# Moving background modulation work between the stages of a one-core decoder layer, and another order of weight rooms in its double gate blocks

## The chip, the cores and the metric

One Trainium2 chip, of which the kernel uses one core. The metric is the time of one execution on the device in microseconds (us). The median of three runs of the kernel before is 1582.16 us.

## The reference

One layer of a decoder trunk for T = 256 tokens of width D = 2048, all in float32. Cut to what matters here:

```
mod = silu(c) @ w_ada + b_ada                  # 2048 x (6 x 2048)
shift1, scale1, gate1, shift2, scale2, gate2 = split(mod, 6)
h = rms_norm(x, norm1_gain) * (1 + scale1) + shift1
proj = h @ w_in                                # q/k/v of three mixers, r, a, and 3 x 2048 gate columns
o_sb  = stick_breaking_attention(q_sb, k_sb, v_sb)         # 6 heads of 128
o_dil = dilated_mixture(q_dil, k_dil, v_dil)               # 3 groups of 2 heads
o_gla = rms_norm(gla_chunked(q, k, v, log_a)) * silu(r)    # 4 heads, value width 256
g = sigmoid(gate columns)                      # 3 x 2048
y = g[0] * (o_sb @ w_br_sb) + g[1] * (o_dil @ w_br_dil) + g[2] * (o_gla @ w_br_gla)
x = x + gate1 * (y @ w_out)
h = rms_norm(x, norm2_gain) * (1 + scale2) + shift2
x = x + gate2 * (swiglu(h, w_ffn_in) @ w_ffn_out)
```

The layer needs shift1 and scale1 at once, gate1 only behind w_out, shift2 and scale2 only at the second norm, gate2 only at the end. So their share of the product with w_ada can be computed at any time before that. This late share is called the background modulation.

## The kernel before

**Products.** Each large product is made of three fp32r matmuls (lines 173 to 175): activations and weights are split into a high part and the rest. A weight tile `raw` (512 KB: two k of 128 rows by 512 columns) is loaded by SP's queue. ScalarE casts it to `whi` (line 165, in pairs line 236), VectorE subtracts to get `wlo` (line 166, in pairs line 222), and TensorE runs twelve matmuls of 512 columns on it, for two halves of the tokens. There are four tiles each of raw, whi and wlo, so the loads, casts and subtractions run some tiles ahead of TensorE. SP, ScalarE and VectorE each work through one queue in order.

**Order.** The program is written block by block, and a planner then lays down the order of each engine's instructions; work inside `prio()` is put earlier than it is written. At run time the order on each engine is fixed.

**Stages** (times of the profiled execution). First groups of k with the first norm, to 239 us. Last group (`LAST`, five k): thirteen projection blocks `proj_block(LAST, b)` of 512 columns, and among them the norms of q and k (`qk_norm`, squares at line 771, product at line 779), their transposes (`qk_turn`, lines 791 and 792), stick-breaking attention (matmuls at line 843, which take what ScalarE makes at line 838), and gated linear attention (line 867 and behind). A projection block is seeded with the earlier groups' sum (copy at line 620) and brought back by a copy (line 632). Two blocks for r to about 419 us. Three gate blocks of the first 512 columns with the dilated mixture, to 493 us. Three double gate blocks `gate_pair` (two times 512 columns each), 494 to 615 us. y blocks 0 to 2 (branch products times gates) to 684, three single gate blocks and y block 3 to 790, three w_out blocks to 850, the fourth with the second norm, then the feed-forward part to the end.

**Double gate blocks.** `fast_products` runs eight pairs of k. Three of them (`GATE_PAIRS`) are fast: seven products in place of eight, from sums of activations (`sums_of_h`) and sums of weights, which VectorE makes at line 222 as well. A split takes its rooms by turns: first those of `more_rooms` (extra tiles whose owners are idle), then the ordinary four whi/wlo. A9/A10 are such extra rooms and hold part of the gated linear output until the transposes of line 1261 have read it; X1/X2 are scratch of `sums_of_h`.

**Background.** `background()` is a generator over three segments (shift2, gate1, scale2). A step issues one load of w_ada on SP (line 517, 512 KB: one k by 1024 columns) into a tile of a ring (`ring["tags"]`: AR0, AR1, and in some stages KC, KD, OD), and where the ring is full it first issues the oldest multiply-add on VectorE ("mac", lines 419 and 421), placed behind the latest split. There are 96 loads and 96 macs. `block` ticks at every second k, `fast_products` twice per pair of k:

```
tick(state["rate"] * pace)         # line 189, pace is 1 in these blocks
tick(2 * state["rate"])            # fast_products, once per pair of k
```

`tick` adds up the rate, and makes a step for each whole number reached. So `state["rate"]` sets how many loads and macs a stage carries; what is left before the second norm is done at once. `RATE_IN` holds from projection block 5, `RATE_MID` from the r blocks, `RATE_LAST` from the last gate blocks. After the background come twelve k of gate2 (`gate2_bg`), beside w_out and the first feed-forward units.

Of the kernel before, what the change touches and what calls it, by code (L numbers as in the profile page):

```python
# [29 lines left out]
N_DIL = 6  # L30
N_GLA = 4
SEG_SHIFT1, SEG_SCALE1, SEG_GATE1, SEG_SHIFT2, SEG_SCALE2, SEG_GATE2 = range(6)
RATE_FIRST, RATE_IN, RATE_MID, RATE_PAIRS, RATE_Y, RATE_LAST = 0.8, 0.8, 0.6, 0.2, 0.5, 0.7

RATES_OP, RATES_FFN, RATE_OUT = (0.9, 0.7, 0.0), (0.75, 0.9, 0.7, 0.6), 0.5
GATE2_CUT = 12
LOOK = 3
DEFER = 4
# [42 lines left out]
def trunk(ctx: ExitStack, tc: tile.TileContext, I, out):  # L81
# [16 lines left out]
    def S(tag, shape, dtype=F32):  # L98
        return slot.tile(shape, dtype, tag=tag, name=nm(tag))
# [7 lines left out]
    def acc_bank(shape=None):  # L107
        return psa.tile(shape or [P, NB], F32, tag="acc", name=nm("acc"))
# [4 lines left out]
    @contextmanager  # L113
    def prio(offset=AHEAD):

        with tc.high_priority(offset=offset):
            start = tc.cur_priority
            yield
            n = tc.cur_priority - start
        tc.cur_priority += n  # L120

    state = {"rate": 0.0}
# [54 lines left out]
    def block(pss, act, src, k0, k1, c0, base=0, w=None, tiles=range(NT), go_on=False, more=False, seeded=False,  # L177
              steps=None, pace=None):

        if w is None:
            w = load_weights(src, k0, k1, c0)
        if pace is None:
            pace = 1.0 if tiles[-1] == NT - 1 else 0.0
        for k in range(k0, k1):
            if (k - k0) % 2 == 0:
                tick(state["rate"] * pace)
            if k - k0 == DEFER and later:  # L190
                with tc.issue_after(state["mm"].ins), prio():
                    later.pop()()
            if steps and k - k0 in steps:
                with tc.issue_after(state["mm"].ins), prio():
                    steps[k - k0]()
            wh, wl = w[k - k0]
            for t in tiles:
                h, l = act(base + k, t)
                mm3(pss[t], h, l, wh, wl, k == k0 and not go_on, k == k1 - 1 and not more, seeded)
# [411 lines left out]
    def proj_block(g, b, w=None, carry=False, steps=None):  # L611
        k0, k1 = GROUPS[g]
        go_on = bool(carried)
        pss = carried.pop() if go_on else [acc_bank() for _ in range(NT)]
        seeded = g == LAST and not go_on
        if seeded:

            with prio():
                for t in range(NT):
                    nc.scalar.copy(pss[t], A[b][:, t, :])  # L620
            go_on = True
        block(pss, h_at, w_in, k0, k1, b * NB, w=w, go_on=go_on, more=carry, seeded=seeded, steps=steps)
        if carry:
            carried.append(pss)
            return
        with prio():
            first = A[b] is None
            if first:
                A[b] = S(f"A{b}", [P, NT, NB])
            for t in range(NT):  # L630
                if first or seeded:
                    nc.scalar.copy(A[b][:, t, :], pss[t])
                else:
                    nc.vector.tensor_add(A[b][:, t, :], A[b][:, t, :], pss[t])
# [126 lines left out]
    def qk_norm(parts):  # L761

        n = sum(h1 - h0 for _, h0, h1, _ in parts)
        ss = small([P, NT, n])
        places, o = [], 0
        for b, h0, h1, _ in parts:
            for t in range(NT):
                for h in range(h0, h1):
                    junk = scr([P, P])
                    i = o + h - h0  # L770
                    nc.scalar.activation(junk, heads(b)[:, t, h, :], AF.Square, accum_out=ss[:, t, i : i + 1])
            places.append(slice(o, o + h1 - h0))
            o += h1 - h0
        r = rsqrt(ss.rearrange("p t h -> p (t h)"), 1.0 / P, [P, NT * n])
        r = r.rearrange("p (t h) -> p t h", t=NT)
        for (b, h0, h1, _), c in zip(parts, places):
            for t in range(NT):
                v = heads(b)[:, t, h0:h1, :]
                nc.vector.tensor_tensor(
                    v, v, r[:, t, c].unsqueeze(2).to_broadcast([P, h1 - h0, P]), op=ALU.mult  # L780
                )
# [269 lines left out]
    def mixture_rows(prob, sm, lse, den, spans):  # L1051
        G = lambda x, g: x[:, :, 2 * g : 2 * g + 2]
        coef = const.tile([P, NT, N_DIL], F32, name="dcoef")
        for g in range(3):
            nc.vector.tensor_mul(G(coef, g), G(sm, g), den)
        nc.vector.reciprocal(coef, coef)
        nc.vector.tensor_mul(coef, coef, lse)
        for h in range(N_DIL):
            p = prob[h // 2][:, h % 2, :]
            for t, (a, b) in enumerate(spans):  # L1060
                state["rows"] = nc.vector.tensor_scalar(p[:, a:b], p[:, a:b], coef[:, t, h : h + 1], None, op0=ALU.mult)
# [73 lines left out]
    def background():  # L1135
        for seg in (SEG_SHIFT2, SEG_GATE1, SEG_SCALE2):
            if seg == SEG_GATE1:
                acc = biased([S(f"T{4 + j}", [P, 2 * NB]) for j in range(2)], seg)
                yield from ada_segment_steps(acc, seg, rows_of("gate1", seg, acc), False)
            else:  # L1140
                acc = S("ada", [P, D])
                yield from ada_segment_steps(halves(acc), seg, columns(seg, acc))
        yield from last_macs()

    bg.append(background())
    state["rate"] = RATE_FIRST
    for b in range(0, 3):
        proj_block(LAST, b)
    state["rate"] = 0.0
    qk_norm(sb_parts)  # L1150
    for b in range(3, 5):
        proj_block(LAST, b)
# [32 lines left out]
    def gate_block(n, br, steps=None):  # L1185
        pss = [acc_bank() for _ in range(NT)]
        c0 = COL_G + br * D + n * NB
        block(pss, h_at, w_in, 0, KC, c0, steps=steps)
        g = S(gtags[n][br], [P, NT, NB])
        with prio():  # L1190
            for t in range(NT):
                if n == 0:
                    nc.scalar.copy(g[:, t, :], pss[t])
                else:
                    nc.scalar.activation(g[:, t, :], pss[t], AF.Sigmoid)
        gates[n, br] = g

    def gate_pair(br, own, other, rooms, raws=()):
        state["more_rooms"], state["more_raws"] = rooms, raws
        c0 = COL_G + br * D + NB  # L1200
        o = fast_products(w_in, c0, c0 + NB, GATE_PAIRS, h_at, h_sums, own, other, ("A0", "A1"), look=LOOK)
        with prio():
            for i in range(2):
                g = S(gtags[1 + i][br], [P, NT, NB])
                for t in range(NT):
                    nc.scalar.activation(g[:, t, :], o[i][t], AF.Sigmoid)
                gates[1 + i, br] = g
# [20 lines left out]
    with prio():  # L1228
        groups = dil_weights()
        mixture_rows(*groups)  # L1230
    gate_block(0, 0)
    ring["tags"] = ("AR0", "AR1", "KC", "KD")
    od, turns = mixture(groups[0])
# [86 lines left out]
    h_sums = sums_of_h()  # L1320
    state["rate"] = RATE_PAIRS
    ring["tags"] = ("AR0", "AR1", "KD")
    gate_pair(0, acc_bank, misc_bank, (("A9", "A10"), ("X1", "X2")))
    gate_pair(1, misc_bank, acc_bank, (("A9", "A10"),), ("X2",))
    gate_pair(2, acc_bank, misc_bank, (("A9", "A10"),))
    ring["tags"] = ("AR0", "AR1", "KC", "KD")
    state["rate"] = RATE_Y
# [339 lines left out]
```

## Time and profile before

| what | before |
|---|---|
| runs | 1583.51, 1582.16, 1581.06 us; median 1582.16 |
| profiled execution | 1581.34 us |
| its span, first to last instruction | 1579.5 us |
| mean granted TensorE clock | 0.999 |
| loads of w_ada into AR0/AR1 | 62 of 512 KB, 5.0 us from issue to landing |
| loads of w_in | 202 of 512 KB, 5.0 us |
| HBM traffic over the span | 254 GB/s |

Lines of the profile name an engine (PE is TensorE, PEld its weight load, DVE VectorE, ACT ScalarE, POOL GpSimd, SPq the queue of SyncE), the line of the kernel, the operation, output<-inputs and shape. In a timeline the first number is the start and the second the duration in us; in brackets at its end stands the idle time before it and what ended it. Starts of matmuls are measured, their ends are modelled, so that a matmul of 0.39 us overlaps the next. In a list of waits the three numbers are the total, the count and the longest, in us.

### The profile page before, as it was taken

The numbers are of one execution on the slowest core, as the hardware profiler recorded it, in microseconds if no ns is written. First come the engines' busy times: TensorE is split into PE (matmuls) and PEld (weight loads), VectorE is DVE, ScalarE is ACT, GpSimd is POOL, SyncE is SP. The second block draws the span as 40 slices with busy tenths as digits, with TensorE's granted clock in tenths as the row PEclk, the third lists the DMA queues.
The fourth block names the chain that finished last, engine by engine and source line by source line (L and its number), as shares of the span: only waits on it lengthen the run. The fifth ranks groups of instructions, "written<-read, shape, count | busy, mean of one in ns | idle before, by whom it ended". The sixth has DMA issues, their size and how long they took to land.

```text
span 1579.5 us, 20270 instructions
## 1 busy us (share of the span) xinstructions
PE 1562.7 (99%) x7177; PEld 1291.9 (82%) x7177; DVE 1407.3 (89%) x1728; ACT 881.9 (56%) x1222; POOL 12.3 (1%) x24
## 2 busy tenths in 40 slices
PE   9999999999999999999999999999999999999998
PEld 7878888788887888888887888888888888888887
DVE  6889997888888899987887889999999999889896
ACT  5654448875765555344434645556565555455553
POOL 1000000000000000000000000000000000000000
PEclk9999999999999999999999999999999999999999
DMA  9999988767778677888998896665566566866664
GB/s 334 359 327 322 336 305 289 252 214 226 253 249 269 217 239 243 304 285 310 315 315 276 305 314 222 196 206 198 191 211 211 173 200 231 289 227 201 225 209 138
DMA packets 196317, 402.26 MB, mean 255 GB/s; under 512 B 13102, under 2 KB 28116, under 8 KB 196216
## 3 DMA queue, kind: packets, MB, share of 16 engines
q1 hardware_dynamic: 194952, 397.75, 74.5%
q0 software_dynamic: 1088, 3.16, 0.5%
q8 instruction: 56, 0.92, 0.2%
q14 instruction: 45, 0.37, 0.1%
q10 hardware_dynamic: 176, 0.07, 0.0%
HBM read 395.68 MB, written 5.24 MB: 254 GB/s over the span
## 4 chain that ended last, share of the span: by engine, by line
PE 83%; DVE 7%; DMA 4%; ACT 3%; issue 2%; SPq 0%; ACTq 0%; DVEq 0%
PE acc L175 20%; PE acc L174 19%; PE acc L173 19%; PE misc L173 7%; PE misc L175 7%; PE misc L174 7%; DMA raw<-w_in 2%; DVE wlo L222 1%; ACT whi L165 1%; DVE wlo L166 1%; PE misc L945 1%; DMA A<-w_ada 1%; DMA OS<-w_ada 1%; DVE KD L222 1%; DVE OD L222 1%
## 5 line engine op out<-in xcount | busy, mean ns | idle before, releaser
L165 ACT CAST whi<-raw 128x1024 fp32r<-128x1024 f32 (+1 forms) x277 | 278.9, 1012 | 284.2 <-PE acc L175 149.8
L166 DVE TENSOR_TENSOR wlo<-raw,whi 128x1024 fp32r<-128x1024 f32 (+1 forms) x277 | 321.0, 1169 | 83.8 <-ACT whi L165 82.3
L173 PE MATMUL acc<-whi,H 128*128 128x512 f32 (+1 forms) x993 | 388.6, 392 | 1.0 <-ACT H L588 0.8
L174 PE MATMUL acc<-wlo,H 128*128 128x512 f32 (+1 forms) x993 | 387.5, 390 | 1.4 <-DVE wlo L166 1.3
L175 PE MATMUL acc<-whi,H 128*128 128x512 f32 (+1 forms) x993 | 387.2, 391 | 0.5 <-DVE H L595 0.4
L174 PEld LDWEIGHTS acc<-wlo,H 128*128 128x128 f32 x993 | 186.6, 188 | 40.1 <-DVE wlo L166 2.7
L175 PEld LDWEIGHTS acc<-whi,H 128*128 128x128 f32 x993 | 186.2, 188 | 40.0 <-DVE H L595 1.4
L173 PEld LDWEIGHTS acc<-whi,H 128*128 128x128 f32 x993 | 186.5, 188 | 39.7 <-ACT H L588 1.3
L236 ACT CAST whi<-raw 128x1024 fp32r<-128x1024 f32 (+1 forms) x144 | 138.9, 975 | 85.7 <-PE acc L175 41.2
L222 DVE TENSOR_TENSOR wlo<-raw,whi 128x1024 fp32r<-128x1024 f32 (+1 forms) x144 | 159.6, 1122 | 13.2 <-ACT whi L236 11.8
L175 PE MATMUL acc<-whi,A 128*128 128x512 f32 x217 | 84.5, 389 | 0.0
L174 PE MATMUL acc<-wlo,A 128*128 128x512 f32 x209 | 81.5, 390 | 1.5 <-DVE wlo L166 1.5
L173 PE MATMUL acc<-whi,A 128*128 128x512 f32 x209 | 81.8, 391 | 0.0
L173 PE MATMUL misc<-whi,H 128*128 128x512 f32 (+1 forms) x208 | 81.0, 389 | 0.0
L175 PE MATMUL misc<-whi,H 128*128 128x512 f32 (+1 forms) x208 | 80.6, 387 | 0.0
L174 PE MATMUL misc<-wlo,H 128*128 128x512 f32 (+1 forms) x208 | 80.5, 387 | 0.0
L421 DVE SCALAR_TENSOR_TENSOR ada<-AR,csil,ada 128x1024 f32<-128x1024 f32 x41 | 52.0, 1279 | 10.7 <-DMA AR<-w_ada 10.7
L222 DVE TENSOR_TENSOR A<-raw,A 128x512 f32<-128x512 f32 (+2 forms) x61 | 55.2, 912 | 0.7 <-ACT A L236 0.2
L175 PEld LDWEIGHTS acc<-whi,A 128*128 128x128 f32 x217 | 40.7, 188 | 8.5
L174 PEld LDWEIGHTS acc<-wlo,A 128*128 128x128 f32 x209 | 39.3, 188 | 10.0 <-DVE wlo L166 2.0
L173 PEld LDWEIGHTS misc<-whi,H 128*128 128x128 f32 x208 | 39.1, 188 | 8.3 <-issue 0.4
L173 PEld LDWEIGHTS acc<-whi,A 128*128 128x128 f32 x209 | 39.2, 188 | 8.0
(665 smaller groups left out, 3005.7 us busy)
## 6 DMA issues: line engine op xcount, KB each, us to landing
raw<-w_in SPq DMA_DIRECT2D x202, 512.0 KB, 5.0
raw<-w_ffn_in SPq DMA_DIRECT2D x135, 512.0 KB, 4.6
raw<-w_ffn_out SPq DMA_DIRECT2D x73, 512.0 KB, 5.4
AR<-w_ada SPq DMA_DIRECT2D x62, 512.0 KB, 5.0
raw<-w_out SPq DMA_DIRECT2D x32, 512.0 KB, 6.5
OS<-w_ada SPq DMA_DIRECT2D x24, 512.0 KB, 6.3
AR<-w_ffn_in SPq DMA_DIRECT2D x22, 512.0 KB, 5.4
KC<-w_ada SPq DMA_DIRECT2D x20, 512.0 KB, 5.6
```

The lines of the kernel that those rows point to most:

```text
L165: state["cast"] = nc.scalar.copy(hi[:, :n, :], raw[:, :n, :])
L166: state["split"] = nc.vector.tensor_tensor(lo[:, :n, :], raw[:, :n, :], hi[:, :n, :].bitcast(F32), op=ALU.subtract)
L173: nc.tensor.matmul(ps, lh, rh, start=start, stop=False, skip_group_check=seeded)
L174: nc.tensor.matmul(ps, lh, rl, start=False, stop=False, skip_group_check=seeded)
L175: state["mm"] = nc.tensor.matmul(ps, ll, rh, start=False, stop=stop, skip_group_check=seeded)
L222: done = nc.vector.tensor_tensor(dst, x, y, op=ALU.subtract)
L236: nc.scalar.copy(hi[:, :n, :], src)
L421: nc.vector.scalar_tensor_tensor(acc, raw, c, acc, op0=ALU.mult, op1=ALU.add)
L945: nc.tensor.matmul(ps[:n, t * N_GLA + h, :].rearrange("p (s l) -> p s l", l=L), at(f, h, t)[:, :n], odd(at(f, h, t)), start=True, stop=True,)
```

## The change

Three things. The background starts with projection block 5 (the sixth) and no longer with block 0. The rates of four stages differ: the three single gate blocks get a rate of their own (0.75 for 0.6), the pairs 0.3 for 0.2, y blocks 0 to 2 0.6 for 0.5, the w_out blocks (0.8, 0.4, 0) for (0.9, 0.7, 0). And each double gate block begins its turn of rooms behind the extra ones, so that its first four splits use the ordinary whi/wlo; in the first of them X1/X2 come ahead of A9/A10.

```
-RATE_FIRST, RATE_IN, RATE_MID, RATE_PAIRS, RATE_Y, RATE_LAST = 0.8, 0.8, 0.6, 0.2, 0.5, 0.7
-RATES_OP, RATES_FFN, RATE_OUT = (0.9, 0.7, 0.0), (0.75, 0.9, 0.7, 0.6), 0.5
+RATE_IN, RATE_MID, RATE_GATES, RATE_PAIRS, RATE_Y, RATE_LAST = 0.8, 0.6, 0.75, 0.3, 0.6, 0.7
+RATES_OP, RATES_FFN, RATE_OUT = (0.8, 0.4, 0.0), (0.75, 0.9, 0.7, 0.6), 0.5
...
     bg.append(background())
-    state["rate"] = RATE_FIRST
     for b in range(0, 3):
         proj_block(LAST, b)
-    state["rate"] = 0.0
     qk_norm(sb_parts)
...
     def gate_pair(br, own, other, rooms, raws=()):
         state["more_rooms"], state["more_raws"] = rooms, raws
+        state["tiles"] = len(rooms) - 1
...
+    state["rate"] = RATE_GATES
     gate_block(0, 0)
...
-    gate_pair(0, acc_bank, misc_bank, (("A9", "A10"), ("X1", "X2")))
+    gate_pair(0, acc_bank, misc_bank, (("X1", "X2"), ("A9", "A10")))
     gate_pair(1, misc_bank, acc_bank, (("A9", "A10"),), ("X2",))
     gate_pair(2, acc_bank, misc_bank, (("A9", "A10"),))
```

More of the change, by code (lines that the diff above doesn't have):

```diff
@@ L32 @@
 SEG_SHIFT1, SEG_SCALE1, SEG_GATE1, SEG_SHIFT2, SEG_SCALE2, SEG_GATE2 = range(6)
-RATE_FIRST, RATE_IN, RATE_MID, RATE_PAIRS, RATE_Y, RATE_LAST = 0.8, 0.8, 0.6, 0.2, 0.5, 0.7
-RATES_OP, RATES_FFN, RATE_OUT = (0.9, 0.7, 0.0), (0.75, 0.9, 0.7, 0.6), 0.5
+RATE_IN, RATE_MID, RATE_GATES, RATE_PAIRS, RATE_Y, RATE_LAST = 0.8, 0.6, 0.75, 0.3, 0.6, 0.7
+RATES_OP, RATES_FFN, RATE_OUT = (0.8, 0.4, 0.0), (0.75, 0.9, 0.7, 0.6), 0.5
 GATE2_CUT = 12
@@ L1145, in trunk @@
     bg.append(background())
-    state["rate"] = RATE_FIRST
     for b in range(0, 3):
         proj_block(LAST, b)
-    state["rate"] = 0.0
     qk_norm(sb_parts)
@@ L1199, in gate_pair @@
         state["more_rooms"], state["more_raws"] = rooms, raws
+        state["tiles"] = len(rooms) - 1
         c0 = COL_G + br * D + NB
@@ L1230, in trunk @@
         mixture_rows(*groups)
+    state["rate"] = RATE_GATES
     gate_block(0, 0)
@@ L1322, in trunk @@
     ring["tags"] = ("AR0", "AR1", "KD")
-    gate_pair(0, acc_bank, misc_bank, (("A9", "A10"), ("X1", "X2")))
+    gate_pair(0, acc_bank, misc_bank, (("X1", "X2"), ("A9", "A10")))
     gate_pair(1, misc_bank, acc_bank, (("A9", "A10"),), ("X2",))
```

## The prediction

> **What bounds the kernel now.** I read the head of the page first: the busy sums, then the chain that ended last, then the groups.
>
> ```profile
> span 1579.5 us, 20270 instructions
> PE 1562.7 (99%) x7177; PEld 1291.9 (82%) x7177; DVE 1407.3 (89%) x1728; ACT 881.9 (56%) x1222; POOL 12.3 (1%) x24
> ...
> PE 83%; DVE 7%; DMA 4%; ACT 3%; issue 2%; SPq 0%; ACTq 0%; DVEq 0%
> ...
> L421 DVE SCALAR_TENSOR_TENSOR ada<-AR,csil,ada 128x1024 f32<-128x1024 f32 x41 | 52.0, 1279 | 10.7 <-DMA AR<-w_ada 10.7
> ```
>
> TensorE is busy 1562.7 of 1579.5 us and carries 83% of the chain. The change removes no instruction, it moves background work: loads of w_ada on SP's queue and the multiply-adds on VectorE (the L421 group; "macs" below). So it can win only from the gaps of TensorE, and lose only by making new ones. The next view is the waits of TensorE; the five rows below are those with waits in the part that the diff touches.
>
> ```profile
> PE acc L174 <- DVE wlo L166: 2.7, 3, 1.5
> ...
> PE misc L867 <- ACT A L792: 1.7, 1, 1.7
> PE acc L173 <- ACT A L236: 1.2, 1, 1.2
> PE misc L843 <- ACT T L838: 1.0, 2, 0.6
> ...
> PE acc L174 <- DVE A L222: 0.5, 1, 0.5
> ```
>
> They are 7.1 us together. Of the first row 0.62 and 1.46 us lie in that part (rows below); the third wait, 0.6 us, lies in the groups ahead of it. So about 6.5 us of waiting, 0.41% of the time, is all that this change can bring. The profiled execution took 1581.34 us (1.84 us around its span), 0.82 us below the median of the three runs, 1582.16 us. I make the sum against 1581.34 and put 0.82 on at the end. About 0.2% (3.2 us) is what a measurement of this kernel can tell from no change.
>
> **Part 1: no background in projection blocks 0 to 2.** Each of these blocks covers five k, with a step at every second (three): 3 x 3 x 0.8 = 7.2 background steps. In the orders of the changed kernel seven macs and five loads are moved behind block 5; the first two AR loads are still issued early. TensorE's own rows and those of the transfer that it waited for:
>
> ```profile
> 251.89 3.11 SPq L517 DMA_DIRECT2D AR<-w_ada  x2
> 255.05 4.39 SPq L151 DMA_DIRECT2D raw<-w_in  x4
> 261.21 1.05 ACT L165 CAST whi<-raw 128x1024 fp32r<-128x1024 f32 x1 [0.36 <-DMA raw<-w_in]
> 262.39 0.39 PE L175 MATMUL acc<-whi,H 128*128 128x512 f32 x1
> 262.62 0.39 PE L173 MATMUL acc<-whi,H 128*128 128x512 f32 x1
> 263.63 0.50 PE L174 MATMUL acc<-wlo,H 128*128 128x512 f32 x1 [0.62 <-DVE wlo L166]
> 240.00:280.00 40.00, 37.65 (x182) 30.94 (x181) 28.45 (x37) 32.54 (x90) 1.04 (x1) 1.00 0.86 289
> ```
>
> Unhindered matmuls start 0.23 us apart (262.39, 262.62), so the gap at 262.62 is 1.01 - 0.23 = 0.78 us. Its weights were loaded at 255.05, directly behind two AR loads that held SP's queue for 3.11 us, in a window where the DMA engines were 86% busy. Without five of the loads of 512 KB this load is issued earlier, and I take the whole 0.78 us as gone; the bounds are 0 (the next load is as late) and 0.78. The moved steps are taken up by the gate blocks and pairs (part 3).
>
> The gap behind the transposes is another matter:
>
> ```profile
> 274.46 1.91 PE L791 MATMUL misc<-ident,A 128*128 128x128 f32 x16
> 276.37 0.59 ACT L620 COPY acc<-A 128x512 f32<-128x512 f32 x1
> 276.89 0.58 ACT L632 COPY A<-acc 128x512 f32<-128x512 f32 x1
> 277.37 0.69 ACT L792 ACTIVATE A<-misc,qgains 128x512 f32<-128x512 f32 x1
> 278.11 0.30 PE L867 MATMUL misc<-H,T 128*32 128x256 f32 x1 [1.74 <-ACT A L792]
> ```
>
> L867 needs a bank that the copy L792 frees, and L792 stands in ScalarE's queue behind a seed (L620) and an eviction (L632) of the projection. In the changed order six matmuls (6 x 0.23 = 1.4 us) come between L791 and L867, but ScalarE has one more cast (1.05 us by the 261.21 row) ahead of L792. Gain at best 1.4 us, at worst 1.4 - 1.05 = 0.35 us; I take 0.6, nearer the lower end because the cast is in the same queue. The two waits at L843 (1.0 us) end with ScalarE's L838; head 0 of the scores is moved forward in the order, which gives between +0.6 (one more copy of the 276.89 kind in ScalarE's way) and -1.0 (both go); I take -0.5.
>
> **Part 2: the rooms of the double gate blocks.** Pair 0 starts here:
>
> ```profile
> 492.61 1.91 PE L1261 MATMUL misc<-ident,A 128*128 128x128 f32 x16
> 494.60 1.04 ACT L236 CAST A<-raw 128x1024 fp32r<-128x1024 f32 x1
> 495.70 0.73 PE L173 MATMUL acc<-A,H 128*128 128x512 f32 x2 [1.18 <-ACT A L236]
> 496.75 1.22 DVE L222 TENSOR_TENSOR A<-raw,A 128x1024 fp32r<-128x1024 f32 x1
> 497.18 0.39 PE L174 MATMUL acc<-X,H 128*128 128x512 f32 x1
> 498.02 0.50 PE L174 MATMUL acc<-A,H 128*128 128x512 f32 x1 [0.46 <-DVE A L222]
> ```
>
> The first split goes to A9/A10, tiles of the gated-linear output whose last readers are the transposes L1261. They end at 492.61 + 1.91 = 494.52; the cast starts at 494.60, the subtraction at 496.75. TensorE loses 1.18 us at 495.70 and 498.02 - 497.18 - 0.23 = 0.61 us at 498.02: 1.8 us. After the change the first four splits use the ordinary whi/wlo tiles, free as the last gate block eats them, and A9/A10 come sixth. The casts then stand well before the transposes in both queues: all 1.8 us should go, with 0 as the other bound if another queue holds the split (VectorE's, next part).
>
> **Part 3: more background in the gate blocks and pairs.** A block of 16 k ticks eight times, a pair sixteen times. That gives 18 for 14.4 steps in the three single gate blocks, 14.4 for 9.6 in the pairs, 14.4 for 12 in y blocks 0 to 2, 9.6 for 12.8 beside w_out. The order of VectorE, counted by splits, says the same: five macs behind before at the first pair, level after the first y block, four ahead in the second.
>
> ```profile
> 397.00:494.00 97.00, 97.00 (x474) 80.70 (x473) 84.05 (x140) 66.98 (x143) 0.00 (x0) 1.00 0.76 256
> 494.00:534.00 40.00, 38.37 (x171) 31.30 (x170) 38.70 (x49) 22.89 (x29) 0.00 (x0) 1.00 0.77 256
> 534.00:575.00 41.00, 40.97 (x181) 33.67 (x180) 36.99 (x44) 23.36 (x27) 0.00 (x0) 1.00 0.67 214
> 575.00:615.00 40.00, 40.00 (x177) 32.85 (x177) 36.36 (x42) 22.33 (x26) 0.00 (x0) 1.00 0.69 231
> DVE A L222 <- DMA raw<-w_in: 5.2, 5, 1.9
> 840.40 1.28 DVE L421 SCALAR_TENSOR_TENSOR OS<-KD,csil,OS 128x1024 f32<-128x1024 f32 x1
> 841.59 1.28 DVE L421 SCALAR_TENSOR_TENSOR T<-KC,csil,T 128x1024 f32<-128x1024 f32 x1
> ```
>
> (Columns: window, its length, then busy time of PE, PEld, DVE, ACT, POOL, the clock, the DMA share, GB/s.) In 397 to 494 VectorE has 97.00 - 84.05 = 12.95 us free and TensorE waits for nothing: three or four more macs cost nothing there; without that cover they would cost 1.19 us each, since macs follow one another by 841.59 - 840.40 = 1.19 us. The pairs are the tight place: VectorE is free for 1.30, 4.01 and 3.64 us in the three windows, 8.95 us in all, 5.2 of them in five waits for raw weights. The order puts one more mac into pair 0, three more into pair 1, one more into pair 2: 5 x 1.19 = 5.95 us. By totals it fits. By place it hardly does: in pair 1 two macs stand directly ahead of the last subtraction of a fast product, and the matmul waits for that. Laying the queue out by hand with these durations and no idle time, VectorE is behind by some 0.2 us in pair 0 and 1.0 us in pair 1. Bounds: 0, if all waits for raw give way, and 5.95, if none does. I take 1.2, near the lower end: the waits are for transfers, at a DMA share of 0.67 to 0.77, and a VectorE that comes later finds them landed. Part 2 and this together: -1.8 + 1.2 = -0.6. The five loads that come with those macs, 2.6 MB in 121 us, are 22 GB/s more on 214 to 256: at that DMA share I put them at nothing, and if they do delay a raw load it is the next rival that they feed. POOL has none of the moved work.
>
> The Trainium skill, VectorE: DVE Perf Modes, section "The DRAIN you can't avoid", says that the next operation doesn't start until the pipe of the one before is empty. By that a mac would cost its whole 1.28 us and five 6.4 instead of 5.95. The rows disagree: the second mac starts 0.09 us before the first ends. I stay with 1.19.
>
> **Part 4: the w_out blocks.**
>
> ```profile
> 806.00:840.00 34.00, 34.00 (x157) 28.13 (x156) 24.91 (x28) 14.60 (x20) 1.10 (x2) 1.00 0.93 320
> 834.49 0.69 DVE L1352 TENSOR_TENSOR A<-A,scr 128x512 f32<-128x512 f32 x1 [3.35 <-DMA A<-x]
> 849.20 1.05 ACT L165 CAST T<-raw 128x1024 fp32r<-128x1024 f32 x1 [2.34 <-DMA raw<-w_out]
> 851.45 0.40 PE L173 MATMUL acc<-whi,A 128*128 128x512 f32 x1
> 853.30 0.50 PE L174 MATMUL acc<-wlo,A 128*128 128x512 f32 x1 [1.46 <-DVE wlo L166]
> ```
>
> The gap is 853.30 - 851.45 - 0.23 = 1.62 us. VectorE stood 3.35 us for a piece of x, queued on SP behind weights while the DMA engines were 93% busy; everything behind it slid, the loads that wait for freed buffers too, and the weights cast at 849.20 were late. In the changed order three loads of x stand two, eight and nine rows earlier on SP, and the last w_ada loads before the w_out weights. I take 1.2 of the 1.62 us as gained; bounds 0 and 1.62. The number of w_ada loads beside w_out stays seven. The y blocks and the four single blocks behind them show no TensorE wait for weights and get about as many macs as before: nothing. From the feed-forward units on the orders are the same but for swaps: within 0.5 us either way.
>
> **Sum.** -0.78 - 0.6 - 0.5 - 0.6 - 1.2 = -3.7 us: 1577.7 in the profiled run, 1578.5 as a median. If the terms miss by half of the way to their bounds, not all to one side, that is some 2.5 us either way: 1576 to 1581 is its own range.
>
> **Rivals.**
> - *VectorE binds the pairs (slower).* For it: 38.70 busy of 40 us in pair 0; pair 1's macs sit ahead of a fast product. If the waits for raw stay as they are, because a later VectorE frees the raw buffers later and so delays the next transfers by as much, the queue's length is the stage's length: the 1.8 us are lost again and the macs add 5.95. With only the first gap and L843 gained: +5.95 - 0.78 - 0.5 = +4.7, so 1586.8. It decides once more than 3 us of the 8.95 us (8.95 - 5.95) can't be filled. Against it: between 534 and 615 TensorE is busy for 80.97 of 81 us now, with VectorE at 91%. The Trainium skill, Perfetto Trace Analysis, section "Identifying the Most-Contended Engine", leans this way: it would judge TensorE by weight loading (82% here), which leaves VectorE with 89% as the engine to relieve. The matmuls' steps of 0.23 us without a break, and 40.00 busy us of 40.00 in the last window, speak against that reading.
> - *The gaps only move (same).* L867 waits as long behind the extra cast, and the w_out loads stay late, since the DMA engines, 93% busy there, set their time and not their place in the queue. Then only 0.78 and 0.5 us stay: 1580.9.
> - *All five gaps close and the macs hide (faster).* -(0.78 + 1.74 + 1.0 + 1.8 + 1.62) = -6.9 us, so 1575.2.
> That the change doesn't do what it says is not likely: the orders show the move; only the two early loads remain.
>
> **How the numbers follow.** Forecast 0.45, VectorE-bound 0.22, gaps move 0.22, all gone 0.11. The forecast lies 0.5 us beyond the 0.2% line, so two thirds of it count as faster: 0.30 + 0.11 = 0.41. Same: 0.15 + 0.22 = 0.37. Slower: 0.22. The range from 1575.5 to 1586.0 takes in the forecast, the moved gaps, half of the best case and the nearer part of the slower one, whose price has 5.95 as its upper bound.
>
> **What would show it.** Right: no TensorE wait near 263; the first pair starts without a wait for an A tile; TensorE waits for L222 by about 1 us inside pair 1; the wait for x at L1352 and the wait of 1.5 us beside it gone. Wrong: several waits for L222 between 500 and 615 with VectorE over 95% busy (VectorE binds); or the wait at L867 still 1.7 us and w_out's weights late (gaps move); or a new wait in a stage that I put at nothing.

## The result, and the profile after

The changed kernel is slower: 1584.4 us median of 20 runs against 1581.8 us of 20 runs of the kernel before, ratio 1.0017 with a 95% interval of 1.001 to 1.0025, so about 2.7 us. The forecast was 3.7 us faster. Its profiled execution took 1583.95 us with a span of 1582.2 us, 2.7 us longer than the span before.

Single executions of one kernel spread over several us (1581.61 to 1588.84 here), so below the verdict on a kernel comes from its ratio, and a profile only tells where its own execution lost or won. One execution of experiment 5 took 4078.72 us and is in no ratio.

The busy sums of the page after:

```profile
PE 1565.0 (99%) x7177; PEld 1291.5 (82%) x7177; DVE 1409.5 (89%) x1728; ACT 881.1 (56%) x1222; POOL 12.7 (1%) x24
```

Nothing is to be seen in these sums. To find the place I took the start of the same (n-th) L173 matmul of 512 columns in both traces. The table lists how the difference, after minus before, grows from stage to stage.

| stage (us before) | after minus before at its end | change in the stage | forecast |
|---|---|---|---|
| to 256, first groups | -0.26 | | |
| projection blocks with q/k work, to 340 | -3.92 | -3.7 | -1.9 |
| gated linear attention, to 412 | -3.89 | 0.0 | 0 |
| second r block and single gate blocks, to 482 | -2.64 | +1.25 | 0 |
| start of pair 0, to 513 | -4.24 | -1.6 | -1.8 |
| the rest of the pairs, to 623 | -1.48 | +2.8 | +1.2 |
| y block 0, to 651 | -1.48 | 0.0 | 0 |
| y blocks 1 and 2, first of the last gate blocks, to 708 | +4.54 | +6.0 | 0 |
| to 821 | +4.67 | +0.1 | 0 |
| end of w_out and second norm, to 879 | +2.84 | -1.8 | -1.2 |
| feed-forward, to the end | +2.62 | -0.2 | 0 |

The waits of TensorE after, those in the part that the diff touches:

```profile
PE acc L174 <- DVE wlo L166: 2.2, 4, 0.8
PE misc L1127 <- DVE T L1122: 1.6, 1, 1.6
PE misc L173 <- DVE A L324: 1.1, 1, 1.1
PE misc L791 <- DVE A L779: 0.9, 1, 0.9
...
PE acc L173 <- ACT whi L236: 0.8, 1, 0.8
PE misc L174 <- DVE A L222: 0.6, 1, 0.6
...
PE misc L173 <- DVE A L1268: 0.3, 1, 0.3
```

The four waits of the first row include one ahead of the part that the diff touches. Of the five rows before, L867, L843 and the two waits for an A tile at the start of pair 0 are gone. New are L1127 and L324 (both in the y blocks), L791, and in the pairs L1268, the cast and another wait for an L222 (at 522.95 us, inside pair 0).

The large loss first. Of the 6.0 us, 2.2 are lost in y block 1 and 3.8 in y block 2 (the same n-th matmuls again, to 669 and to 690 us before). This is the timeline of SP, VectorE, ScalarE and TensorE around y block 1's loads of w_br_gla in the changed kernel:

```profile
644.69 0.89 SPq L151 DMA_DIRECT2D raw<-w_br_gla  x2
...
651.33 0.34 SPq L517 DMA_DIRECT2D AR<-w_ada  x1
651.72 0.94 SPq L151 DMA_DIRECT2D raw<-w_br_gla  x2
...
650.02 1.28 DVE L421 SCALAR_TENSOR_TENSOR T<-AR,csil,T 128x1024 f32<-128x1024 f32 x1
...
659.42 1.05 ACT L165 CAST whi<-raw 128x1024 fp32r<-128x1024 f32 x1 [4.76 <-DMA raw<-w_br_gla]
...
661.78 0.50 PE L174 MATMUL acc<-wlo,A 128*128 128x512 f32 x1 [0.77 <-DVE wlo L166]
```

and this SP's row for the same four loads in the kernel before:

```profile
641.47 9.49 SPq L151 DMA_DIRECT2D raw<-w_br_gla  x4
```

The ring tile AR is free only when its mac is done: the mac of 650.02 ends at 651.30, the load goes at 651.33. Behind it stand the last two loads of w_br_gla. ScalarE waits 4.76 us for the first of them, and TensorE 0.77 us for the weights made from it (and 0.41 us for earlier ones at 657.58). So here SP stands for a mac of VectorE, and TensorE for a load of SP.

In y block 2 SP stands in the same way, but TensorE's waits are others:

```profile
668.42 0.89 SPq L151 DMA_DIRECT2D raw<-w_br_gla  x2
675.02 1.88 SPq L517 DMA_DIRECT2D AR<-w_ada  x2
676.99 0.90 SPq L151 DMA_DIRECT2D raw<-w_br_gla  x2
...
683.86 1.05 ACT L165 CAST whi<-raw 128x1024 fp32r<-128x1024 f32 x1 [5.85 <-DMA raw<-w_br_gla]
...
673.71 1.28 DVE L421 SCALAR_TENSOR_TENSOR ada<-AR,csil,ada 128x1024 f32<-128x1024 f32 x1
...
675.24 1.28 DVE L421 SCALAR_TENSOR_TENSOR ada<-AR,csil,ada 128x1024 f32<-128x1024 f32 x1
...
677.63 1.28 DVE L324 TENSOR_TENSOR A<-misc,A 128x512 fp32r<-128x512 f32 x2
...
684.94 1.23 DVE L166 TENSOR_TENSOR wlo<-raw,whi 128x1024 fp32r<-128x1024 f32 x1 [0.16 <-ACT whi L165]
686.32 1.23 DVE L166 TENSOR_TENSOR wlo<-raw,whi 128x1024 fp32r<-128x1024 f32 x1
687.46 0.42 DVE L1122 TENSOR_TENSOR T<-T,T 128x256 fp32r<-128x256 f32 x1
...
678.37 0.50 PE L173 MATMUL misc<-whi,OD 128*128 128x512 f32 x1 [1.07 <-DVE A L324]
...
687.93 0.39 PE L1127 MATMUL misc<-T,ones_r 128*128 128x256 f32 x1 [1.65 <-DVE T L1122]
```

SP issues two loads of w_br_gla by 669.31 and then nothing for 5.7 us, until the mac of 673.71 ends at 674.99. The last two loads of w_br_gla go at 676.99, behind two AR loads, and ScalarE waits 5.85 us for them. TensorE, though, waits 1.65 us for L1122, a subtraction for gate1's rows, which VectorE has in its queue behind the two subtractions of these weights. These came late for VectorE by only 0.16 us at 684.94 and about as much at 686.32; the rest is VectorE's own work. Its load in y block 2, before and after (columns as in the prediction's windows):

```profile
668.45:689.75 21.30, 21.30 (x100) 17.73 (x98) 19.90 (x24) 9.78 (x11) 0.00 (x0) 1.00 0.87 310
669.17:694.29 25.12, 22.41 (x103) 18.12 (x102) 24.81 (x30) 10.81 (x14) 0.00 (x0) 1.00 0.92 317
```

VectorE is busy for 24.81 of 25.12 us; in the kernel before, no subtraction for gate1's rows and one mac fewer fall into this stage. The 1.07 us at 678.37 are VectorE's own too: L324 stands in its queue behind the mac of 675.24 and one more.

### The profile page after: what moved, and what is told of

It is laid out like the page before. It is cut to its first block, busy times and chain, and to the rows that moved or that the text cites. A ratio compares the mean times of both kernels' runs of the same rounds, so it can differ in the third digit from the quotient of the medians.

```text
span 1582.2 us, 20278 instructions
## 1 busy us (share of the span) xinstructions
PE 1565.0 (99%) x7177; PEld 1291.5 (82%) x7177; DVE 1409.5 (89%) x1728; ACT 881.1 (56%) x1222; POOL 12.7 (1%) x24
## 4 chain that ended last, share of the span: by engine, by line
PE 79%; DVE 7%; DMA 6%; ACT 4%; issue 3%; SPq 0%; ACTq 0%; DVEq 0%
PE acc L175 18%; PE acc L174 18%; PE acc L173 18%; PE misc L174 6%; PE misc L175 6%; PE misc L173 6%; DMA raw<-w_br_gla 2%; DMA raw<-w_in 2%; ACT whi L165 2%; DVE wlo L222 1%; DVE A L222 1%; DVE wlo L166 1%; DMA raw<-w_br_sb 1%; PE acc L576 1%; PE misc L945 1%
## 5 line engine op out<-in xcount | busy, mean ns | idle before, releaser
L173 PE MATMUL acc<-whi,H 128*128 128x512 f32 x1006 | 393.6, 393 | 1.8 <-ACT H L588 0.8
L174 PE MATMUL acc<-wlo,H 128*128 128x512 f32 x1006 | 392.4, 390 | 0.8 <-DVE wlo L166 0.7
L175 PE MATMUL acc<-whi,H 128*128 128x512 f32 x1006 | 392.4, 391 | 0.5 <-DVE H L595 0.4
L173 PEld LDWEIGHTS acc<-whi,H 128*128 128x128 f32 x1006 | 188.8, 188 | 41.4 <-ACT whi L236 1.5
L175 PEld LDWEIGHTS acc<-whi,H 128*128 128x128 f32 x1006 | 188.7, 188 | 40.6 <-DVE H L595 1.4
L222 DVE TENSOR_TENSOR wlo<-raw,whi 128x1024 fp32r<-128x1024 f32 (+1 forms) x142 | 158.0, 1128 | 11.8 <-ACT whi L236 10.6
L173 PE MATMUL acc<-whi,A 128*128 128x512 f32 x209 | 81.9, 392 | 0.1
L175 PE MATMUL misc<-whi,H 128*128 128x512 f32 (+1 forms) x204 | 79.1, 388 | 0.0
L173 PE MATMUL misc<-whi,H 128*128 128x512 f32 (+1 forms) x204 | 78.7, 389 | 0.0
L222 DVE TENSOR_TENSOR A<-raw,A 128x512 f32<-128x512 f32 (+2 forms) x63 | 57.4, 917 | 0.5
L236 ACT CAST whi<-A 128x1024 fp32r<-128x1024 f32 x28 | 29.5, 1054 | 37.6 <-DVE A L222 35.1
L173 PEld LDWEIGHTS acc<-whi,A 128*128 128x128 f32 x209 | 39.3, 188 | 8.5 <-ACT whi L165 0.6
```

Source lines behind the costliest of these rows:

```text
L173: nc.tensor.matmul(ps, lh, rh, start=start, stop=False, skip_group_check=seeded)
L174: nc.tensor.matmul(ps, lh, rl, start=False, stop=False, skip_group_check=seeded)
L175: state["mm"] = nc.tensor.matmul(ps, ll, rh, start=False, stop=stop, skip_group_check=seeded)
L222: done = nc.vector.tensor_tensor(dst, x, y, op=ALU.subtract)
L236: nc.scalar.copy(hi[:, :n, :], src)
```

## The experiments

All were run beside the kernel before on the same chip, in five rounds; a ratio is to that kernel, with its 95% interval.

**1. The y blocks' rate back.** In the changed kernel:

```
-... RATE_PAIRS, RATE_Y, RATE_LAST = ... 0.3, 0.6, 0.7
+... RATE_PAIRS, RATE_Y, RATE_LAST = ... 0.3, 0.5, 0.7
```

> The changed kernel with the rate of y blocks 0 to 2 back at 0.5 (12 background steps in place of 14.4); all else as changed. In the profiles the changed kernel is level with or ahead of the one before until the second y block and then loses 6.0 us up to the first of the last gate blocks. Theory A (the y blocks' own rate: more w_ada loads stand between their weight loads on SP's queue): most of the 6.0 us is gone, so about 2 to 4 us faster than before, 1578 to 1580. Theory B (the background's lead from earlier stages, which brings the gate1 rows and the scale2 macs into y block 2): the loss stays at 4 us or more, 1582 to 1584.

Measured 1.0002 (0.9993 to 1.001): the loss is gone, no gain is left. Its profiled execution, 1578.58 us (the lowest of its runs, median 1581.13), gains as far as y block 0 like the changed kernel and loses 1.1 us in the y blocks, not 6.0. Theory A's time was forecast lower; its place was right.

**2. Only the rooms,** put into the kernel before:

```
+        state["tiles"] = len(rooms) - 1
-    gate_pair(0, ..., (("A9", "A10"), ("X1", "X2")))
+    gate_pair(0, ..., (("X1", "X2"), ("A9", "A10")))
```

> The kernel before with only the order of rooms changed (first four splits of each pair to the ordinary rooms, X1/X2 ahead of A9/A10 in the first). If the start of the first pair was held by the room alone: its 1.8 us go and nothing new comes, 1580. Rival (VectorE binds the pairs, so that what is won at the start is waited for later in the pairs): 1581.5 to 1582, with waits for L222 inside the pairs.

Measured 1.0008 (0.9997 to 1.0019): no gain. The start's gap is gone, but pair 0 pays later (line 1269 here is 1268 elsewhere):

```profile
514.11 0.77 PE L173 MATMUL misc<-whi,T 128*128 128x512 f32 x1 [2.62 <-DVE A L1269]
```

The first fast product needs four banks of the `misc` kind. The last of them holds transposes of the gated linear output until VectorE's L1269 has read it, and with the splits ahead of schedule the planner put that L1269 behind them. The rival's bookkeeping was right, its place not: a bank and not a split.

**3. Only the late start,** in the kernel before:

```
-    state["rate"] = RATE_FIRST
     for b in range(0, 3):
```

> The kernel before with only the background's start moved behind projection block 2; every other rate and the rooms as before, so that all later stages run some seven macs behind. Up to 320 us it should gain the changed kernel's 3.6 us. Theory A: the y blocks keep their rate and lose nothing, about 1578.5 to 1579.5, less 1.0 if the wait in the second r block comes along. Theory B (position of the background decides): a loss of some us shows in or behind the y blocks though their rate is unchanged, 1580 or more.

Measured 1.0068 (1.0051 to 1.0084), 10.8 us slower. Theory A's time is missed. Theory B's words (a loss in or behind the y blocks, 1580 or more) take it in, but neither theory had its cause. The first part gains 3.7 us and the y blocks lose nothing, as theory A has it. But SP's order now has 85 w_ada loads before the first of w_out, for 92 in the kernel before; the rest moves into the w_out blocks, and there (SP, VectorE and TensorE; lines 1427, 1350 and 1351 are 1428, 1351 and 1352 elsewhere)

```profile
815.19 17.01 SPq L151 DMA_DIRECT2D raw<-w_out  x8
832.25 0.47 SPq L517 DMA_DIRECT2D A<-w_ada  x1
832.77 2.50 SPq L1427 DMA_DIRECT2D A<-x  x3
...
841.13 0.69 DVE L1351 TENSOR_TENSOR A<-A,scr 128x512 f32<-128x512 f32 x1 [9.32 <-DMA A<-x]
...
842.47 0.79 PE L173 MATMUL acc<-whi,A 128*128 128x512 f32 x1 [7.58 <-DVE scr L1350]
```

three pieces of x stand behind eight weight loads and a w_ada load. VectorE waits 9.32 us for x and TensorE 7.58 us for VectorE (in the slowest of its six runs, 1595.91 us). What a late start leaves over has to be placed before w_out; the other rates of the change do that (96 loads stand before w_out in it).

**4. All w_ada loads on another queue.** In the changed kernel:

```
-                    nc.sync.dma_start(raw, w_ada[...])       # line 517
+                    nc.gpsimd.dma_start(raw, w_ada[...])
```

> The changed kernel with the background's w_ada loads (line 517) issued by GpSimd's queue in place of SP's; no rate and no order on VectorE is meant to change. If the loss in the y blocks comes from SP's queue standing at a w_ada load that waits for its ring tile, with weight loads behind it, this takes it away: the 6.0 us fall below 2, and the time comes to 1577 to 1580. If the transfers' bandwidth or VectorE's queue is what is short, the loss stays as it is: 1583 to 1585. If GpSimd's issue costs VectorE or the transfers something, it shows as longer macs or loads.

Measured 1.0069 (1.0055 to 1.0084). The time says nothing on the y blocks, because this edit costs elsewhere; among TensorE's waits stand

```profile
PE misc L173 <- DVE A L1268: 4.0, 1, 4.0
...
PE misc L348 <- POOL ident masks.py:199: 3.1, 1, 3.1
```

the bank of experiment 2 and GpSimd's setup work behind its loads at the start (in the kernel before, L348 waits 2.5 us for a load). From 651 to 708 us the loss is 2.7 in place of 6.0, and TensorE waits for no weight there. Experiment 12 does it for the y blocks alone.

**5. The changed kernel again**, unchanged.

> The changed kernel once more, beside the next three on one chip. Expected 1.001 to 1.0025 of the kernel before. Theory A says it is slower than the same kernel with the y blocks at rate 0.5, which came out at 1.0002 of before, by 1 to 4 us.

Measured 1.0018 (1.0007 to 1.0029). The profile loses in the same places, in the y blocks 7.3 us. The excess over 6.0 has a reason of its own, shown in the last section. The second r block and the single gate blocks lose 0.1 us here, for 1.25 in the first profile of the same kernel.

**6. Only the y blocks' rate**, in the kernel before: `RATE_Y` 0.6 for 0.5.

> The kernel before with only the rate of y blocks 0 to 2 at 0.6. Theory A (the y blocks' rate by itself puts w_ada loads between the weight loads on SP): 2 to 6 us slower, with TensorE waits for wlo of the y blocks between 650 and 690. Theory B (rate and lead together): within 1 us of before, no waits there.

Measured 0.9992 (0.9982 to 1.0001). Theory A falls: the rate by itself costs nothing. It costs only in a background that is ahead.

**7. The changed kernel with the old rooms**, the reverse of experiment 2's diff.

> The changed kernel with the old order of rooms. With only the order of rooms changed in the kernel before, the 1.8 us at the start of the first pair went and 2.8 us came back at its first fast product, where TensorE waits for a bank that VectorE's L1268 frees late. If that exchange holds here too, this kernel has the start's wait back (1.2 and 0.5 us) and fewer waits inside the first pair: within 1 us of the changed kernel, 1583 to 1585. If the rooms are a gain: 2 us slower than the changed kernel.

Measured 0.9997 (0.9987 to 1.0008), about 3 us faster than the changed kernel, which neither expected. Its profile has the start's gaps back (1.40 and 0.88 us) and loses 5.1 us in y block 2, where TensorE waits 1.81 us for L324, and behind that wait seven matmuls start 0.43 us apart for 0.23, some 1.4 us more (last section). In y block 1 it loses nothing, and in the rest of the pairs 0.2 us, for 2.8 of the changed kernel.

**8. Late start, paid for in the single gate blocks.** In the changed kernel, old rooms and

```
-... RATE_GATES, RATE_PAIRS, RATE_Y, ... = ... 0.75, 0.3, 0.6, ...
-RATES_OP = (0.8, 0.4, 0.0)
+... RATE_GATES, RATE_PAIRS, RATE_Y, ... = ... 0.85, 0.2, 0.5, ...
+RATES_OP = (0.9, 0.7, 0.0)
```

> Late start as in the changed kernel, the moved steps given to the single gate blocks alone (rate 0.85: 20.4 steps for 14.4); pairs 0.2, y blocks 0.5, w_out (0.9, 0.7, 0) and the rooms as before; 96.8 steps ahead of the last gate blocks' rest, so that nothing is left over for w_out. If the losses come from the rates of pairs and y blocks: the first part's 3.6 us less 1.0 for the second r block stay, 1578 to 1580, faster than both kernels. If VectorE in the gate blocks (12.95 us free, six more macs are 7.1 us) fills up: new waits for wlo there, 1582 or more.

Measured 0.9983 (0.9973 to 0.9992), median 1579.11 us: faster than both, as expected. The y blocks lose nothing. (The 96.8 steps of the expectation were counted wrong: 91 w_ada loads stand before w_out, one fewer than before.)

**9. The pairs' rate back**, in the changed kernel: `RATE_PAIRS` 0.2 for 0.3.

> The changed kernel with the pairs back at rate 0.2 (9.6 steps for 14.4). So far: the y blocks' rate 0.6 alone costs the kernel before nothing, and costs the changed kernel some 2.5 us. If it is the lead of the background from the pairs that makes it dear (the gate1 segment ends, and its rows begin, inside y block 2), the y blocks lose under 2 us here, and the macs inside the pairs go too: 1579.5 to 1581.5. If the lead isn't the cause: the waits between 650 and 690 stay, 1583 or more.

Measured 1.0002 (0.9993 to 1.001): the loss is gone, though the y blocks keep 0.6. Its profile has no wait of TensorE at all in them, and none at the turn from pair 1 to pair 2. It doesn't gain because x comes late beside w_out again, and TensorE waits 2.72 us at 825 for the residual behind it:

```profile
824.10 0.69 DVE L1352 TENSOR_TENSOR A<-A,scr 128x512 f32<-128x512 f32 x1 [3.79 <-DMA A<-x]
```

**10. Experiment 8 with the changed rooms.**

> The kernel with the late start and the single gate blocks at 0.85 (0.9983 of before) with the changed order of rooms, both parts. If the rooms close the start's gap (2.9 us in that kernel's profile) and nothing comes back: 1576 to 1577.5. If what they win is lost inside the pairs or later, as the changed kernel with old rooms (0.9997 against 1.0018) suggests: 1579 to 1582.

Measured 0.9972 (0.9963 to 0.9982), median 1576.73 us of 9 runs: the fastest of all, 0.28% below the kernel before. Its SP queue in y block 2, and VectorE's load in the gate blocks (the columns are those of the prediction's windows):

```profile
661.80 6.11 SPq L151 DMA_DIRECT2D raw<-w_br_gla  x4
668.74 2.81 SPq L517 DMA_DIRECT2D AR<-w_ada  x2
...
397.00:494.00 97.00, 97.00 (x476) 80.68 (x475) 88.18 (x143) 65.21 (x137) 0.00 (x0) 1.00 0.84 280
```

All four loads of w_br_gla go ahead of the two AR loads, and the macs moved there hide in the gate blocks: VectorE 88.18 for 84.05 us, TensorE busy throughout.

**11. Experiment 8 with only X1/X2 first**, without the other part of the rooms.

> The same kernel with only X1/X2 put ahead of A9/A10 in the first pair, the extra rooms still used first. The first split then waits for no transpose, the second does, one product (2.7 us) later, which is longer than the gap of 1.4 us. If the gap is the room's: 2 to 3 us faster than with the old order, 1576 to 1577.5. If VectorE's order there (the rest of L1268, the first fast product) sets the pair's start in any case: 1579.

Measured 0.9985 (0.9976 to 0.9993), the same as experiment 8. The wait moves on by one product and a bank wait follows, so the gap isn't closed by the order of the two extra rooms alone:

```profile
495.89 0.50 PE L174 MATMUL acc<-A,H 128*128 128x512 f32 x1 [1.26 <-DVE A L222]
```

**12. Another queue in the y blocks alone.** In the changed kernel:

```
+    state["queue"] = nc.gpsimd
     y_block(0, ...)
     y_block(1)
     y_block(2)
+    state["queue"] = nc.sync
...
-                    nc.sync.dma_start(raw, w_ada[...])       # line 517
+                    state.get("queue", nc.sync).dma_start(raw, w_ada[...])
```

> The changed kernel with the w_ada loads of y blocks 0 to 2 alone issued by GpSimd's queue; the planner moves a few macs behind splits there. In the changed kernel SP issues two AR loads at 675 us, held until their macs have freed the tiles, and the last two w_br_gla loads stand behind them; in the kernels that lose nothing there all four w_br_gla loads stand ahead. If SP's queue is the cause, TensorE's waits for wlo and whi between 650 and 690 go (2.5 to 3.5 us of the 6 to 7) and the wait at L1127, which comes from VectorE's order behind the same late weights, shrinks: 1578.5 to 1581.5. If VectorE or the bandwidth is the cause, nothing changes: 1583.5 to 1585.

Measured 1.0 (0.9991 to 1.0009) against 1.0017 and 1.0018 of the changed kernel: 2.7 us by SP's queue. (The planner also moves a few macs there, so this is not SP's share to the tenth.) TensorE's waits from 615 to 700 us are one of 0.2 us in the kernel before, and in the changed one those shown above: 1.6 us for L1122, 1.2 for wlo (two waits) and 1.1 for L324. In this one they are

```profile
PE misc L1127 <- DVE T L1122: 1.5, 1, 1.5
PE misc L173 <- DVE A L324: 0.8, 1, 0.8
```

With SP free, its four loads of w_br_gla go in one row in y block 1 as in y block 2 (SP's timeline), and the waits for weights vanish:

```profile
638.35 9.76 SPq L151 DMA_DIRECT2D raw<-w_br_gla  x4
...
660.95 8.70 SPq L151 DMA_DIRECT2D raw<-w_br_gla  x4
```

The two y blocks lose 3.4 us in place of 6.0: y block 1 nothing for 2.2, y block 2 3.4 for 3.8. The wait for L1122 stays with SP free, so it belongs to VectorE's work and order: VectorE has no idle time from 674.51 to L1122 at 685.04. The wait for L324 stays at 0.8 us, but behind another engine: VectorE is idle for 1.39 us before it, for ScalarE's L323, which stands behind a cast that waits 3.76 us for w_br_gla. So 2.7 us are shown to come from SP's queue; most of what TensorE still loses, in y block 2, goes with VectorE's load there, and no run takes that alone away.

## Why the prediction was wrong

**The step that failed** is the sentence in part 4: "The y blocks and the four single blocks behind them show no TensorE wait for weights and get about as many macs as before: nothing." The stage lost 6.0 us, 2.3 us more than the whole forecast gain. I had looked at the waits that existed, and the macs were not "about as many": part 3 itself counts 14.4 steps for 12 there, and a VectorE that gets from level to four ahead in the second y block; by the traces VectorE does 17 macs for 14 from 615 to 690 us. They got no price. What I had not done either is the rule by which I costed the other parts: to see what stands behind each moved instruction on its queue. A background load waits on SP for its ring tile, that for a mac, and the mac is placed behind a split. With the pairs at 0.3 the background reaches the y blocks far enough ahead that ring loads fall between the weights of y blocks 1 and 2, and gate1's rows into y block 2; with the y blocks at 0.6 there are enough of them. Experiments 1 and 9 take away either and most or all of the loss goes (1.1 and 0.0 us are left in the stage); experiment 6 shows that the rate alone is harmless, and 12 shows SP's share, 2.7 us, nearly all of it in y block 1. That the rest, in y block 2, is VectorE's load fits its 24.81 busy of 25.12 us, but is argued and not shown. Which of the planner's choices places the ring loads there was not traced further.

**Part 1** had the right sign and half the size: -3.7 against -1.9. The wait near 263 is gone as forecast. L867 was under-rated:

```profile
274.44 1.05 ACT L165 CAST whi<-raw 128x1024 fp32r<-128x1024 f32 x1
275.39 0.59 ACT L620 COPY acc<-A 128x512 f32<-128x512 f32 x1
275.91 1.84 ACT L792 ACTIVATE A<-misc,qgains 128x512 f32<-128x512 f32 x3
...
276.14 0.39 PE L175 MATMUL acc<-whi,H 128*128 128x512 f32 x1
276.65 0.30 PE L867 MATMUL misc<-H,T 128*32 128x256 f32 x1
```

The cast did come ahead of L792, but two of the copies that stood there before had moved ahead too (one seed is left between), and L792 starts at 275.91 in place of 277.37; the gap shrinks from 1.95 to 0.28 us. Both waits at L843 went (1.0 forecast as 0.5).

**The r blocks** stood in no term of the sum. By the same reshuffling the transposes of the dilated q and k came forward, to where VectorE's L779 stands behind a subtraction whose weights were late:

```profile
413.36 1.23 DVE L166 TENSOR_TENSOR wlo<-raw,whi 128x1024 fp32r<-128x1024 f32 x1 [1.14 <-ACT whi L165]
414.50 1.02 DVE L779 TENSOR_TENSOR A<-A,tiny 128x256 f32<-128x256 f32 x2
...
414.98 0.44 PE L791 MATMUL misc<-ident,A 128*128 128x128 f32 x2 [0.86 <-DVE A L779]
```

1.25 us are lost in this profile, a third of part 1's gain. It is no steady loss: experiment 5, the same kernel, loses 0.1 us there and has no such wait.

**Part 2** held at its place: no wait at the pair's start, 1.6 us won of 1.8. **Part 3** was put at 1.2 us for the added macs, and the pairs lost 2.8 us. The bank wait on L1268 (0.3 us here, 2.6 in experiment 2) had no place in it, and in pair 1 VectorE fills up altogether. The window of pair 1, of the changed kernel and then of experiment 7, which has the same macs and the old rooms:

```profile
534.00:575.00 41.00, 39.93 (x173) 32.14 (x173) 41.00 (x48) 22.14 (x25) 0.00 (x0) 1.00 0.72 225
534.00:575.00 41.00, 40.47 (x179) 33.17 (x178) 40.70 (x49) 24.09 (x28) 0.00 (x0) 1.00 0.71 230
```

In the changed kernel VectorE is busy for 41.00 of 41.00 us (36.99 before), and the raw tiles that it frees late make the next cast late: TensorE loses 1.35 us at the turn to pair 2. The slower rival looks right in kind there, with 2.8 of its 5.95 us. The Trainium skill's Perfetto Trace Analysis, section "Identifying the Most-Contended Engine", points to VectorE by its occupancy, and for this window the trace agrees, 41.00 us against 32.14 of weight loading. But experiment 7 loses only 0.2 us in the rest of the pairs with VectorE at 40.70 us: a nearly full VectorE need not cost TensorE anything, and by these profiles the 2.8 us are not the macs' alone but the macs' together with the new rooms. The prediction priced the two apart. As the mechanism for the whole change the rival was wrong: it had the pairs losing more than they win from their start, which by the table they do by 1.2 us, and the loss that decides lies behind them.

**Part 4's** w_out term was right: -1.8 for -1.2, the wait for x at L1352 gone. One count in it was not: between the first and the last load of w_out stand 11 w_ada loads before and 7 after, not seven in both, so fewer loads beside the weights may have a share in the gain. The **feed-forward** was right too.

On the **rooms** something stays open. From 482 to 623 us, the start and the rest of the pairs together, the changed kernel loses 1.2 us with the new rooms (1.9 in experiment 5) and 0.5 with the old ones (experiment 7): what they win at the start comes back inside the pairs. With the pairs at 0.2 it is the other way: experiment 10 wins 0.4 us there with the new rooms, experiment 8 loses 2.1 with the old. The ratios say the same, 0.9997 without them for 1.0017, and 0.9972 with them for 0.9983 (intervals that overlap). That the rooms pay where the pairs have few macs and cost where they have many would fit these four. It doesn't fit experiment 2, which lost 2.3 us there with few macs, by the wait for the bank and half clock behind it.

## What to carry to other kernels

A background load on the queue of the weights is more than its bytes: while it waits for its buffer, every load behind it waits too, so count for each stage which of its weights stand behind a load whose buffer an engine frees late. Move background work to the stage with idle time on the engine that does it (12.95 us of VectorE in the gate blocks), not in small parts to all stages. And where a planner orders the queues, a change of rate is a change of order everywhere behind it: compare the whole order, and not only the count of moved work.

## What the runs showed of the hardware

A wait of TensorE can cost more than itself. In experiment 5's profile the wait at L1127 is 2.08 us long, and behind it TensorE runs at half clock for some 3.4 us:

```profile
687.02 0.39 PE L1127 MATMUL misc<-T,ones_r 128*128 128x256 f32 x1 [2.08 <-DVE T L1122]
...
687.47 0.63 PE L174 MATMUL acc<-wlo,A 128*128 128x512 f32 x1
687.90 0.63 PE L175 MATMUL acc<-whi,A 128*128 128x512 f32 x1
...
687.00:691.00 4.00, 3.98 (x11) 3.21 (x12) 4.00 (x4) 2.78 (x4) 0.00 (x0) 0.57 0.97 303
```

The granted clock is 0.57 over this window, and matmuls start 0.43 us apart for 0.23: eight of them are 1.6 us more. The same wait of 1.65 us in the first profile of this kernel left the clock at 1.00. One of 1.81 us (experiment 7) and one of 2.62 us (experiment 2) lowered it, one of 2.72 us (experiment 9) did not. So waits of like length can cost 1.6 us more or not, which may be part of the spread of the times; that was not measured. The Trainium skill, TensorE: Matmul & The Clock Gate, section "What's actually happening", has the clock fall to half after an idle window of about 3.4 us that runs freely; the half is what the rows show, but here gaps below 3.4 us were enough.
